# Seven products of halves for the prompt's down projection of a ConvFFN layer

## The chip, the cores and the metric

The kernel runs on one core of one Trainium2 chip. The metric is the time of one execution in device microseconds. The profile of one execution gives the span from its first to its last instruction, which is a little shorter than that time.

## The reference

The reference is one step of a hybrid attention layer, for a prompt of 1024 tokens and a sample of 32, with D_MODEL = 1024 and D_FF = 2816. All inputs and outputs are float32. What the change touches is the end of the layer, the ConvFFN with its residual:

```python
def _post_norm(x, h, gate, g, b):
    y = DEEPNORM_ALPHA * x.astype(jnp.float32) + gate.astype(jnp.float32) * h.astype(jnp.float32)
    mu = jnp.mean(y, axis=-1, keepdims=True)
    var = jnp.mean(jnp.square(y - mu), axis=-1, keepdims=True)
    return ((y - mu) * lax.rsqrt(var + LN_EPS) * g + b).astype(x.dtype)

    # in _conv_ffn
    h = jax.nn.silu(conv) * b
    return jnp.einsum('btf,fd->btd', h, w_down), a_pad[:, -(CONV_WIDTH - 1):]

    # in _layer
    f_out, conv_state = _conv_ffn(u2, conv_prev, w_up, conv_w, conv_b, w_down)
    x = _post_norm(x, f_out, g2, ln2_g, ln2_b)
```

## The kernel before

Stages follow one another: conditioning and input projection, attention, output projection with the first norm (from line 991), up projection with the convolution (from line 1071), and down projection with the second norm (from line 1115). A float32 product is made of three products of a reduced format: each operand is split into a high part (a cast on ScalarE, line 86) and a low part (a subtraction, on VectorE unless another engine is given, line 87), and `mm3` sums high x high, high x low and low x high. The profile shows these products under line 80.

The up projection writes h, transposed, into 22 tiles `hT[j]` of 128 partitions (features) and 1056 columns (1024 tokens of the prompt and 32 of the sample). Each of its 22 steps has two halves, and each half is 72 products. GpSimd (POOL) does only small copies there (lines 1087, 1088, 1093, 1094).

The down projection is `token_products("wd", ...)` (line 871). It goes through three groups of token blocks of 128, `[0, 1, 2, 8]`, `[3, 4, 5]` and `[6, 7]`, where block 8 is the sample. In each group it runs over all 22 tiles of features, and reads `w_down` anew from DRAM, 512 KB for a feature tile. `prepare` (line 880) runs two steps ahead and splits the tokens (`wdt`), the weights (`wdw`) and, in group 0, the sample (`wds`). A block of the prompt takes six products a step (two column halves of 512 by three parts), the sample four. What is left to do for a finished group (multiplying with the gate, adding the residual, statistics, scaling, storing) is handed out in pieces over the next group's steps (list `rest`). The residual, alpha x (x1 x ln1_g + ln1_b), is made in `residual` (lines 1134 to 1141): a load of x1 from the DRAM buffer `dx1`, then eight GpSimd operations of 256 columns for a block. `norm` and `scale` (lines 1146 to 1159) take VectorE, and one GpSimd power for the inverse root (`rstd`, line 978). In the last group `finish` (line 1161) shares the columns of a block among VectorE, ScalarE and GpSimd.

Each engine works through its own queue in order. A scheduler lays the order of the queues out when the program is built, from the order of the code and its own estimate of times, except in `manual_schedule` blocks, where the code's order is kept. Waits between engines are semaphores. Loads and most stores are issued by SP, in order too.

Of the kernel before, what the change touches and what calls it, by code (L numbers as in the profile page):

```python
# [51 lines left out]
def layer_kernel(ctx: ExitStack, tc: tile.TileContext, a: dict, o: list):  # L52
# [1062 lines left out]
    with pool("pf") as pf:  # L1115
# [3 lines left out]
        g2p, ag, ab, lng, lnb = [pt_(n, n, 1) for n in ("g2p", "ag", "ab", "lng", "lnb")]  # L1119
        g2s = pt_("g2s", "g2s", 1, (TS, D))  # L1120
        res = {}

        def begin2(gi, blocks):
            if gi == 0:
                for t, src in ((ag, a["ln1_g"]), (ab, a["ln1_b"]), (g2p, dgate[1][0:1]), (lng, a["ln2_g"]), (lnb, a["ln2_b"])):
                    nc.sync.dma_start(t, src.to_broadcast([P, D]))
                nc.sync.dma_start(g2s, dgate[1][1:2].to_broadcast([TS, D]))
                for t in (ag, ab):
                    nc.vector.tensor_scalar(t, t, ALPHA, None, ALU.mult)
            for b in blocks:  # L1130
                if b < NB:
                    residual(b, pt_(f"rs{b}", "rs", 3))

        def residual(b, r):
            n = rows(b)
            res[b] = r
            nc.sync.dma_start(r, dx1[b * P:b * P + n])
            for c0 in range(0, D, 256):
                c = slice(c0, c0 + 256)
                nc.gpsimd.tensor_tensor(r[:, c], r[:, c], ag[0:n, c], ALU.mult)  # L1140
                nc.gpsimd.tensor_tensor(r[:, c], r[:, c], ab[0:n, c], ALU.add)

        def evacuate2(gi, accs):
            ys, st = {}, {}

            def norm(b):
                y, n = ys[b], rows(b)
                nc.vector.tensor_tensor(y, y, res[b], ALU.add)
                st[b] = moments(y, n)

            def scale(b):
                y, n = ys[b], rows(b)
                mu, rstd = st[b]
                dst = y_p[0, b * P:(b + 1) * P] if b < NB else y_s[0]
                for h in range(2):
                    c = slice(h * 512, (h + 1) * 512)
                    nc.vector.scalar_tensor_tensor(y[:, c], y[:, c], mu, lng[0:n, c], ALU.subtract, ALU.mult)
                    nc.vector.scalar_tensor_tensor(y[:, c], y[:, c], rstd, lnb[0:n, c], ALU.mult, ALU.add)
                    nc.sync.dma_start(dst[:, c], y[:, c])

            def finish(b, acc, d):

                y = ys[b]
                st, mv = cp.tile([P, 2, 6], F32, name="st", tag="st", bufs=3), small("mv", 2, 3)
                for h in range(2):
                    c = slice(h * 512, (h + 1) * 512)
                    nc.vector.tensor_tensor(y[:, c], acc[h], g2p[:, c], ALU.mult)
                    nc.vector.tensor_tensor(y[:, c], y[:, c], res[b][:, c], ALU.add)
                    nc.vector.bn_stats(st[:, h], y[:, c])
                    yield  # L1170
                mu, rstd = spread(st, mv, P)
                nmr = small("nmr")
                nc.gpsimd.tensor_scalar(nmr, mu, rstd, -1.0, ALU.mult, ALU.mult)
                yield
                for c in (slice(0, d // 2), slice(d // 2, d)):
                    nc.vector.scalar_tensor_tensor(y[:, c], y[:, c], mu, lng[:, c], ALU.subtract, ALU.mult)
                    nc.vector.scalar_tensor_tensor(y[:, c], y[:, c], rstd, lnb[:, c], ALU.mult, ALU.add)
                    nc.sync.dma_start(y_p[0, b * P:(b + 1) * P, c], y[:, c])
                for c0 in range(d, D, 256):
                    c = slice(c0, c0 + 256)  # L1180
                    nc.scalar.activation(y[:, c], y[:, c], AF.Identity, bias=nmr, scale=rstd)
                    nc.gpsimd.tensor_tensor(y[:, c], y[:, c], lng[:, c], ALU.mult)
                    nc.gpsimd.tensor_tensor(y[:, c], y[:, c], lnb[:, c], ALU.add)
                nc.scalar.dma_start(y_p[0, b * P:(b + 1) * P, d:D], y[:, d:D])
                yield

            if gi == 2:
                steps = {}
                for b, acc in accs:
                    ys[b] = pt_(f"yo{b}", "y", 4)  # L1190
                    steps[b] = finish(b, acc, 768 if b == 7 else 256)
                with tc.manual_schedule(engines={nc.vector.engine, nc.gpsimd.engine}):
                    for b in (6, 6, 6, 7, 6, 7, 7, 7):
                        next(steps[b])
                return []
# [71 lines left out]
```

## Time and profile before

| what | us |
|---|---|
| median of 3 runs (lowest, highest) | 1599.0 (1595.2, 1604.36) |
| profiled execution, its own time | 1596.38 |
| its span, first to last instruction | 1594.1 |
| mean granted TensorE clock in it | 0.985 of full speed |
| up projection ends, down projection begins | 1297.9 |
| last product of the down projection ends | 1575.1 |

Engines are PE (TensorE), PEld (its weight loads), DVE (VectorE), ACT (ScalarE), POOL (GpSimd) and SP (which issues most transfers). Times in rows are microseconds from the start of the span, unless marked ns. A row names line, engine, operation, output <- inputs by the program's names, and shapes (partitions x columns). `x4` is a count. In square brackets stands the idle time before an instruction and what ended it. A row of windows has the stretch, its length, the busy time (and count of instructions) of PE, PEld, DVE, ACT and POOL, the granted TensorE clock, the busy share of the transfer engines and what they moved in GB/s.

### The profile page before, as it was taken

How to read it: one execution, taken by the hardware profiler on the slowest of the kernel's cores; microseconds unless marked ns; L12 is line 12 of the kernel's file. 1: busy time of each engine (PE TensorE's matmuls, PEld its weight loads, DVE VectorE, ACT ScalarE, POOL GpSimd, SP SyncE). 2: the span in 40 equal slices, each digit the busy share in tenths (PEclk: the TensorE clock that was granted, in tenths of full speed). 3: DMA queues.
4: the chain of work that ended last, by engine and by line, in shares of the span. 5: the costliest groups of instructions: out<-in, count | busy, mean ns of one | idle time of the engine just before them, and what ended most of it. 6: DMA issues, size and time to landing. Idle time of an engine off the chain costs nothing.

```text
span 1594.1 us, 22475 instructions
## 1 busy us (share of the span) xinstructions
PE 1513.3 (95%) x8657; PEld 1266.8 (79%) x8657; DVE 798.5 (50%) x1552; ACT 569.0 (36%) x1123; POOL 365.5 (23%) x496
## 2 busy tenths in 40 slices
PE   6999999988999999899899999999999999997985
PEld 4677778755646777777799999999999988876874
DVE  4522325733536899557852333233323345377495
ACT  3211211244637788545532121112111233332342
POOL 0002014744413343134300000000000005054052
PEclk9999999998999999999999999999999999999998
DMA  9523312579764433445411111111111135344362
GB/s 270 164 95 111 94 46 107 147 194 240 196 185 119 126 77 96 125 162 207 140 54 41 53 40 53 41 53 40 54 41 54 40 129 205 106 149 135 132 207 83
DMA packets 166796, 183.83 MB, mean 115 GB/s; under 512 B 7458, under 2 KB 131907, under 8 KB 166691
## 3 DMA queue, kind: packets, MB, share of 16 engines
q1 hardware_dynamic: 158642, 155.84, 32.3%
q0 software_dynamic: 7760, 26.04, 5.6%
q8 instruction: 68, 1.11, 0.3%
q10 hardware_dynamic: 288, 0.52, 0.1%
q14 instruction: 38, 0.30, 0.1%
HBM read 151.94 MB, written 22.05 MB: 109 GB/s over the span
## 4 chain that ended last, share of the span: by engine, by line
PE 80%; DVE 7%; DMA 4%; issue 2%; POOL 2%; SPq 2%; ACT 2%; POOLq 0%; DVEq 0%; ACTq 0%
PE up L80 21%; PE upc L80 10%; PE wd L80 6%; PE wo L80 4%; PE po L80 3%; PE Sf L80 2%; PE ptf L114 2%; PE Sd L80 2%; PE pod L80 1%; POOL rs L1140 1%; SPq L171 1%; PE wd2y L80 1%; PE wd2x L80 1%; DMA wrfq<-in_w_in 1%; DMA adan<-in_w_ada 1%
## 5 line engine op out<-in xcount | busy, mean ns | idle before, releaser
L1093 POOL COPY cvo<-row 128x2 f32<-128x2 f32 x22 | 20.2, 918 | 385.4 <-ACT row L1091 385.4
L86 ACT CAST wdt<-h 128x384 fp32r<-128x384 f32 (+1 forms) x66 | 31.5, 478 | 160.4 <-PE wd5y L80 70.6
L1140 POOL TENSOR_TENSOR rs<-rs,ag 128x256 f32<-128x256 f32 x32 | 40.1, 1279 | 148.3 <-DMA rs<-dx 125.5
L625 POOL TENSOR_SCALAR wf<-wf,rs 128x128 f32<-128x128 f32 (+7 forms) x64 | 47.4, 745 | 109.2 <-DVE rs L591 71.9
L87 DVE TENSOR_TENSOR wdt<-h,wdt 128x384 fp32r<-128x384 f32 (+1 forms) x66 | 36.7, 556 | 67.8 <-ACT wdt L86 67.7
L1090 ACT COPY row<-up 128x352 f32<-128x352 f32 x44 | 17.8, 458 | 135.3 <-PE up L80 135.3
L1098 ACT ACTIVATE cv<-cv 128x1058 f32<-128x1058 f32 x22 | 24.0, 1089 | 95.5 <-DVE cv L1097 95.5
L590 ACT ACTIVATE wf<-wf,lo 128x128 f32<-128x128 f32 (+7 forms) x64 | 49.5, 776 | 18.3 <-DVE lo L587 16.0
L86 ACT CAST wh<-wr 128x512 fp32r<-128x512 f32 x40 | 24.3, 621 | 85.2 <-DMA wr<-in_w_in 19.3
L590 ACT ACTIVATE wd<-wd,lo 128x128 f32<-128x128 f32 (+7 forms) x64 | 49.6, 776 | 13.9 <-DVE lo L587 11.9
L80 PE MATMUL po<-ptpf,vf 128*64 128x256 f32 (+1 forms) x320 | 53.9, 374 | 0.5 <-DVE ptpf L615 0.4
L87 DVE TENSOR_TENSOR wh<-wr,wh 128x512 fp32r<-128x512 f32 x40 | 28.6, 738 | 51.1 <-ACT wh L86 51.1
L587 DVE CUSTOM_DVE_ANT_0 wf<-Sf,nb 128x512 f32<-128x512 f32 (+3 forms) x64 | 36.9, 589 | 28.5 <-PE Sf L80 21.3
L114 PE MATMUL ptf<-cst,wf 128*128 128x128 f32 x288 | 47.8, 287 | 1.1 <-POOL wf L625 0.7
L114 PEld LDWEIGHTS ptf<-cst,wf 128*128 128x128 f32 x288 | 32.2, 144 | 18.6 <-issue 9.3
L1103 DVE TENSOR_TENSOR h<-up,cv 128x352 f32<-128x352 f32 x44 | 21.0, 520 | 45.1 <-PE up L80 44.0
L80 PEld LDWEIGHTS po<-ptpf,vf 128*64 128x64 f32 x320 | 29.0, 138 | 18.0 <-issue 6.7
L650 POOL TENSOR_SCALAR wd<-wd,rs,lam 128x128 f32<-128x128 f32 (+7 forms) x32 | 26.5, 827 | 64.4 <-DVE rs L591 63.4
L1104 DVE TENSOR_TENSOR h<-upc,cv 128x320 f32<-128x320 f32 x22 | 10.8, 492 | 57.5 <-PE upc L80 57.5
L587 DVE CUSTOM_DVE_ANT_0 wd<-Sd,zero 128x512 f32<-128x512 f32 (+3 forms) x64 | 36.6, 583 | 1.7 <-PE Sd L80 1.3
L80 PE MATMUL pod<-ptpd,vd 128*128 128x256 f32 (+1 forms) x160 | 35.2, 362 | 0.4 <-ACT sq L667 0.3
L80 PEld LDWEIGHTS pod<-ptpd,vd 128*128 128x128 f32 x160 | 29.2, 191 | 4.4 <-ACT sq L667 0.9
(2698 smaller groups left out, 5032.9 us busy)
## 6 DMA issues: line engine op xcount, KB each, us to landing
wr<-in_w_in SPq DMA_DIRECT2D x20, 512.0 KB
adam<-in_w_ada SPq DMA_DIRECT2D x32, 256.0 KB
adan<-in_w_ada SPq DMA_DIRECT2D x32, 256.0 KB
ga<-in_w_ada SPq DMA_DIRECT2D x16, 512.0 KB
out<-z POOLq DMA_DIRECT2D x12, 512.0 KB, 4.0
x<-in_x_prompt SPq DMA_DIRECT2D x8, 512.0 KB
nb<-dcump SPq DMA_DIRECT2D x8, 512.0 KB
xp<-in_x_prompt SPq DMA_DIRECT2D x8, 512.0 KB
```

The source lines that it names most:

```text
L80: nc.tensor.matmul(out, l, r, start=start, stop=stop, **k)
L86: nc.scalar.copy(hi, src)
L87: (eng or nc.vector).tensor_tensor(lo, src, f(hi), ALU.subtract)
L114: nc.tensor.transpose(out, in_, ident[:n, :n])
L587: nc.vector.tensor_tensor_reduce(w[:, c], S[:, 0:n], t, -1.0, lo, ALU.add, ALU.min, lo_)
L590: nc.scalar.activation(w[:, 0:ext], w[:, 0:ext], AF.Exp, bias=lo, scale=-1.0, accum_out=sm)
L625: nc.gpsimd.tensor_scalar(w, w, rs, 1.0, ALU.mult, ALU.mult)
L650: nc.gpsimd.tensor_scalar(e1, e1, r1, lam, ALU.mult, ALU.mult)
L1093: nc.gpsimd.tensor_copy(cvo[:, 0, :, j], row[:, T:T + 2])
L1098: nc.scalar.activation(c[:, 0:L], c[:, 0:L], AF.Silu)
L1103: nc.vector.tensor_tensor(h[:, cs], accs[g], c[:, cs], ALU.mult)
L1140: nc.gpsimd.tensor_tensor(r[:, c], r[:, c], ag[0:n, c], ALU.mult)
```

## The change

The prompt's down projection is no longer three groups of blocks over 22 feature tiles. Tokens, features and output columns are each cut in halves (512 tokens, 11 feature tiles, 512 columns), and seven products of halves (phases 0 to 6), each over 11 steps `k` and four blocks of tokens, give the four quarters of the output, with sums of halves as operands (a scheme of Winograd's kind: seven products where eight would be due). Sums of h are made on VectorE or GpSimd in six tiles `xq`, in the raw weight tiles or in place in `hT`; sums of weights are nested, each made from the one before, and kept in `hT[11 + k][:, 0:512]` (`yk`) from phase 2 on. The result's halves are collected in `y0` (tokens 0 to 511) and `y1` (512 to 1023).

The sample's 32 tokens are multiplied in phases 0, 1, 3 and 5, two products a step. After phase 4 `y0` is complete: it is gated, gets the residual (both GpSimd, 1024 columns), is normalized and stored during phase 5. After phase 5 come the parts of `y1` known by then, and the sample's end; after phase 6 `finish` for four blocks. The last three steps of phase 6 are held back and done block by block.

The residual is prepared in the up projection, in 36 steps of 256 columns by a block (one before each half from the second half on), and stored in a new DRAM buffer `dres`. The output's PSUM pool is a new one with six banks for the products and two for the sample. `token_products`, `gated` and `weights` stay for the output and up projections.

```diff
+    dres = dp.tile([TT, D], F32, name="dres")
...
+        def residuals():
+            steps = [(c0, b) for c0 in range(0, D, RW) for b in range(9)]
+            def load(i):
+                c0, b = steps[i]
+                if b == 0:
+                    gb[c0] = pe.tile([P, 2, RW], F32, name=f"gb{c0}", tag="gb", bufs=2)
+                    for x, n in enumerate(("ln1_g", "ln1_b")):
+                        nc.sync.dma_start(gb[c0][:, x], a[n][:, c0:c0 + RW].to_broadcast([P, RW]))
+                    nc.gpsimd.tensor_scalar(gb[c0], gb[c0], ALPHA, 0.0, ALU.mult, ALU.add)
+                r = pe.tile([P, RW], F32, name=f"rr{c0}{b}", tag="rr", bufs=2)[0:rows(b)]
+                nc.sync.dma_start(r, dx1[b * P:b * P + rows(b), c0:c0 + RW])
+                return r
...
+                nc.gpsimd.tensor_tensor(r, r, gb[c0][0:n, 0], ALU.mult)
+                nc.gpsimd.tensor_tensor(r, r, gb[c0][0:n, 1], ALU.add)
+                nc.gpsimd.dma_start(dres[b * P:b * P + n, c0:c0 + RW], r)
...
+    psum("psd", m=6, po=1, ms=1)
...
-        token_products("wd", w_dn, NJ, hT, begin2, evacuate2, pf, nheld=4)
...
+        LOADS = [((1, 0), None), ((1, 1), None), ((0, 1), (0, 0)), ((0, 0), None), (None, (1, 1)), ((1, 1), (0, 1)), (None, (1, 0))]
+        def load(n):
...
+            raw = (px.tile if n % 3 == 2 else pw.tile)([P, 2, 512], F32, name=f"xt{i}{k}", tag="raw", bufs=1 if n % 3 == 2 else 2)
...
+        def left(n):
...
+            if i == 0:
+                nc.vector.tensor_tensor(xq[k], hq(0, 1, k), hq(1, 1, k), ALU.add)
+                nc.gpsimd.tensor_tensor(xq[k], xq[k], hq(0, 0, k), ALU.subtract)
+        def prepare(n):
...
+            pl = px if n % 4 < 2 else pw
+            hi = pl.tile([P, 2, 512], F32R, name=f"oh{i}{k}", tag="wh", bufs=2)
+            lo = pl.tile([P, 2, 512], F32R, name=f"ol{i}{k}", tag="wl", bufs=2)
+            yk = hq(1, 0, k)
+            if i == 1:
+                nc.gpsimd.tensor_tensor(raw[:, 0], hq(1, 0, k), xq[k], ALU.subtract)
+                split(hi, lo, raw)
+            else:
+                if i == 2:
+                    nc.vector.tensor_tensor(raw[:, 0], hq(0, 1, k), hq(1, 1, k), ALU.add)
+                    nc.gpsimd.tensor_tensor(yk, raw[:, 1], x2, ALU.subtract)
+                if i in (4, 6):
+                    nc.gpsimd.tensor_tensor(yk, x2, yk, ALU.subtract)
+                if i == 5:
+                    nc.gpsimd.tensor_tensor(raw[:, 1], raw[:, 1], x2, ALU.subtract)
...
+                split(hi[:, 1], lo[:, 1], r)
+                split(hi[:, 0], lo[:, 0], l)
+                if i == 3:
+                    nc.gpsimd.tensor_tensor(l, l, hq(0, 1, k), ALU.subtract)
...
+        def gate_and_add(y, b):
+            nc.gpsimd.tensor_tensor(y, y, consts["g2p"], ALU.mult)
+            nc.gpsimd.tensor_tensor(y, y, res[b], ALU.add)
...
+        def norm(b):
+            mu, rstd = moments(y0[b], P)
+            nc.scalar.activation(y0[b], y0[b], AF.Identity, bias=nmr_of(mu, rstd), scale=rstd)
+        def scale(b):
+            y = y0[b]
+            nc.vector.tensor_tensor(y, y, consts["lng"], ALU.mult)
+            nc.vector.tensor_tensor(y, y, consts["lnb"], ALU.add)
+            nc.sync.dma_start(y_p[0, b * P:(b + 1) * P], y)
...
+        def before_last(b):
+            load_residual(4 + b)
+            gate_and_add(y1[b], 4 + b)
...
+        def finish(b, acc):
...
+            nc.vector.tensor_tensor(t, acc, consts["g2p"][:, C0], ALU.mult)
+            nc.vector.tensor_tensor(y[:, C0], y[:, C0], t, ALU.add)
+            nc.vector.bn_stats(st[:, 0], y[:, C0])
...
+            nc.scalar.activation(y[:, C1], y[:, C1], AF.Identity, bias=nmr, scale=rstd)
+            nc.gpsimd.tensor_tensor(y[:, C1], y[:, C1], consts["lng"][:, C1], ALU.mult)
+            nc.gpsimd.tensor_tensor(y[:, C1], y[:, C1], consts["lnb"][:, C1], ALU.add)
+            nc.vector.scalar_tensor_tensor(y[:, C0], y[:, C0], mu, consts["lng"][:, C0], ALU.subtract, ALU.mult)
+            nc.vector.scalar_tensor_tensor(y[:, C0], y[:, C0], rstd, consts["lnb"][:, C0], ALU.mult, ALU.add)
...
+        for i in range(NPH):
+            acc = [b1(f"wd{i}{b}", "m") for b in range(4)]
...
+            for k in range(NK):
+                n = i * NK + k
+                load(n + 3)
+                left(n)
+                prepare(n + 2)
...
+                while rest and NK * (left_ - len(rest)) < left_ * (k + 1):
+                    rest.pop(0)()
...
+                elif i in (4, 5):
+                    nc.vector.tensor_tensor(y1[b][:, C0], y1[b][:, C0], acc[b], ALU.add)
+            if i in (4, 5):
+                for b in range(4):
+                    y = (y0, y1)[i - 4]
+                    nc.vector.tensor_tensor(y[b][:, C1], y[b][:, C1], y1[b][:, C0], ALU.add)
...
+                rest += [load_consts]
+                for b in range(4):
+                    rest += [lambda b=b: gate_block(b), lambda b=b: norm(b), lambda b=b: scale(b)]
+            if i == 5:
+                rest += [lambda b=b: before_last(b) for b in range(4)] + [sample_end]
```

## Rows read from the trace of the kernel before

**Rows 1.** The page's first part: busy time, share and instructions of each engine.

```profile
PE 1513.3 (95%) x8657; PEld 1266.8 (79%) x8657; DVE 798.5 (50%) x1552; ACT 569.0 (36%) x1123; POOL 365.5 (23%) x496
```

**Rows 2.** Windows by stage: up projection, three groups of the down projection, tail.

```profile
760.00:1297.87 537.87, 533.51 (x3312) 526.97 (x3311) 202.80 (x277) 124.20 (x205) 41.48 (x104) 1.00 0.18 54
...
1297.87:1409.10 111.23, 110.12 (x486) 90.68 (x486) 53.52 (x76) 39.89 (x73) 23.89 (x24) 1.00 0.47 163
1409.10:1509.40 100.30, 91.69 (x391) 73.59 (x391) 64.96 (x84) 32.34 (x45) 36.89 (x36) 0.97 0.42 144
1509.40:1575.10 65.70, 61.25 (x265) 49.09 (x264) 58.54 (x79) 26.18 (x38) 20.83 (x20) 1.00 0.50 168
1575.10:1594.10 19.00, 2.66 (x12) 1.88 (x10) 9.21 (x16) 2.19 (x4) 8.80 (x12) 0.71 0.15 55
```

**Rows 3.** The chain in order of time, down projection: start, length, what.

```profile
1459.01 2.72 PE wd L80 x12
```

**Rows 4.** Waits in 1405:1575: who <- for whom, total, times, longest.

```profile
POOL rs L1140 <- DMA rs<-dx: 125.5, 2, 69.4
...
DVE yo L1158 <- POOL rstd L978: 11.6, 1, 11.6
...
PE wd L80 <- DVE wdw18l L87: 8.6, 1, 8.6
```

**Rows 5.** Timeline of GpSimd, undisturbed operations of 1024 and of 256 columns.

```profile
743.09 2.39 POOL L87 TENSOR_TENSOR wow17l<-wow17r,wow17h 128x1024 fp32r<-128x1024 f32 x1 [0.66 <-ACT wow17h L86]
...
1320.46 2.82 POOL L1140 TENSOR_TENSOR rs<-rs,ag 128x256 f32<-128x256 f32 x4 [22.77 <-DVE wds L87]
```

**Rows 6.** Timeline of VectorE while GpSimd is idle.

```profile
1549.09 0.42 DVE L87 TENSOR_TENSOR wdt<-h,wdt 128x256 fp32r<-128x256 f32 x1
1549.42 1.22 DVE L87 TENSOR_TENSOR wdw213l<-wdw213r,wdw213h 128x1024 fp32r<-128x1024 f32 x1
...
1569.59 0.69 DVE L1167 TENSOR_TENSOR yo<-wd6x,g2p 128x512 f32<-128x512 f32 x1 [0.83 <-PE wd6x L80]
...
1571.04 0.69 DVE L1169 BATCH_NORM_STATS2 st<-yo 128x6 f32<-128x512 f32 x1
```

**Rows 7.** Costliest groups, page: ScalarE casts of 512 columns, busy and mean ns.

```profile
L86 ACT CAST wh<-wr 128x512 fp32r<-128x512 f32 x40 | 24.3, 621 | 85.2 <-DMA wr<-in_w_in 19.3
```

**Rows 8.** Windows of three stretches in which GpSimd is busy, columns as in rows 2.

```profile
1325.60:1344.40 18.80, 18.80 (x85) 15.57 (x84) 14.01 (x14) 7.49 (x14) 18.75 (x18) 1.00 0.51 175
...
1419.90:1432.40 12.50, 12.50 (x56) 10.33 (x56) 11.15 (x20) 4.77 (x8) 12.50 (x3) 1.00 0.41 138
1442.10:1451.50 9.40, 2.48 (x11) 1.71 (x10) 8.76 (x5) 1.46 (x2) 7.56 (x12) 0.92 0.11 44
```

**Rows 9.** Groups by line in 1325.6:1344.4, VectorE and GpSimd (six splits of 1024).

```profile
L87 DVE TENSOR_TENSOR wdt<-h,wdt 128x384 fp32r<-128x384 f32 x4 | 3.1, 767 | 4.0 <-ACT wdt L86 4.0
L87 DVE TENSOR_TENSOR wds<-h,wds 128x32 fp32r<-128x32 f32 x4 | 2.9, 721 | 0.0
L87 DVE TENSOR_TENSOR wdw09l<-wdw09r,wdw09h 128x1024 fp32r<-128x1024 f32 x1 | 1.8, 1755 | 0.0
...
L1141 POOL TENSOR_TENSOR rs<-rs,ab 128x256 f32<-128x256 f32 x11 | 11.7, 1089 | 0.0
L1140 POOL TENSOR_TENSOR rs<-rs,ag 128x256 f32<-128x256 f32 x7 | 8.2, 1201 | 0.0
```

**Rows 10.** Timelines of VectorE and GpSimd, four operations stretched each.

```profile
1442.74 8.81 DVE L1158 SCALAR_TENSOR_TENSOR yo<-yo,rstd,lnb 128x512 f32<-128x512 f32 x4 [11.58 <-POOL rstd L978]
...
1418.89 13.56 POOL L1140 TENSOR_TENSOR rs<-rs,ag 128x256 f32<-128x256 f32 x4
```

**Rows 11.** Timeline of GpSimd in the tail.

```profile
1575.01 0.55 POOL L978 TENSOR_TENSOR rstd<-rstd,mhalf 128x1 f32<-128x1 f32 x1 [34.64 <-DVE rstd L977]
1575.67 0.26 POOL L1173 TENSOR_SCALAR nmr<-mv,rstd 128x1 f32<-128x1 f32 x1
...
1585.79 0.72 POOL L1183 TENSOR_TENSOR yo<-yo,lnb 128x256 f32<-128x256 f32 x1
```

More of the change, by code (lines that the diff above doesn't have):

```diff
@@ L34 @@
 BIG = 3.0e38
+RW = 256
 C_ID = 0
@@ L1074, in layer_kernel @@
         L = ROW - 2
+        def residuals():
[10 more added lines that the diff above has]
+                return r
+            gb = {}
+            nxt = load(0)
+            yield
+            for i, (c0, b) in enumerate(steps):
+                r, n = nxt, rows(b)
+                nc.gpsimd.tensor_tensor(r, r, gb[c0][0:n, 0], ALU.mult)
+                nc.gpsimd.tensor_tensor(r, r, gb[c0][0:n, 1], ALU.add)
+                nc.gpsimd.dma_start(dres[b * P:b * P + n, c0:c0 + RW], r)
+                if i + 1 < len(steps):
+                    nxt = load(i + 1)
+                yield
+        resid = residuals()
         for j in range(NJ):
@@ L1077, in layer_kernel @@
             for s in range(2):
+                if j or s:
+                    next(resid, None)
                 _, hi, lo = first_up[s] if j == 0 else up_weights(j, s)
@@ L1112, in layer_kernel @@
     up_.__exit__(None, None, None)
-    with pool("pf") as pf:
+    psum("psd", m=6, po=1, ms=1)
+    NK = NJ // 2
+    NPH = 7
+    HELD = 3
+    C0, C1 = slice(0, 512), slice(512, 1024)
+    with pool("px") as px, pool("pf") as pf:
         def pt_(name, tag, bufs, shape=(P, 1024), dt=F32):
             return pf.tile(list(shape), dt, name=name, tag=tag, bufs=bufs)
[L1119 to L1195, printed above, removed]
-            for b, acc in accs:
-                y = pt_(f"yo{b}", "y", 4)
-                ys[b] = y[0:rows(b)]
-                gated(y, b, acc, g2p if b < NB else g2s)
-                if b == 8:
-                    residual(b, g2s)
-            return [lambda b=b, g=g: g(b) for b, _ in accs for g in (norm, scale)]
-        token_products("wd", w_dn, NJ, hT, begin2, evacuate2, pf, nheld=4)
@@ new lines, in layer_kernel, with late, load_residual, load_consts @@
+        SAMPLE = {0: 0, 1: 1, 3: 0, 5: 1}
+        def late(name, shape=(P, 1024)):
+            return pt_(name, "xq", 6, shape)
+        def load_residual(b):
+            res[b] = late(f"rs{b}")
+            nc.sync.dma_start(res[b][0:rows(b)], dres[b * P:b * P + rows(b)])
+        consts = {}
+        def load_consts():
+            for n, src in (("g2p", dgate[1][0:1]), ("lng", a["ln2_g"]), ("lnb", a["ln2_b"])):
+                consts[n] = late(n)
+                nc.sync.dma_start(consts[n], src.to_broadcast([P, D]))
```

121 lines of the change are left out of this document (added).

## The prediction

> **What bounds the kernel now.** I read the page first: TensorE is busy 95% of the span [rows 1], so only less TensorE work or fewer holes in it can shorten the kernel. Then the windows by stage [rows 2]. The three groups of the down projection take 111.2, 100.3 and 65.7 us, 277.2 in all, and the tail after its last product 19.0. The chain in order of time gives the price of one product: twelve in 2.72 us, so 0.2267 us each [rows 3]. The groups hold 22 x (22 + 18 + 12) = 1144 products, 259.3 us; the other 17.9 us are holes. The waits name the largest [rows 4]: TensorE stood 8.6 us for a weight split on VectorE (wdw18l), which was queued behind a scaling that waited 11.6 us for a GpSimd result (rstd), and GpSimd was then busy with the residual (L1140). In the up projection TensorE is full (533.5 of 537.9 us) and GpSimd nearly empty (41.5) [rows 2].
>
> **TensorE's share of the change.** Seven products of 11 k steps, four blocks and three parts are 924; the sample adds 88, as before. That is 1012 products or 229.4 us, 29.9 less than now. Phases 0, 1, 3 and 5 (with the sample) have 154 products, 34.9 us each; 2, 4 and 6 have 132, 29.9 us. The loop bounds fix these counts, so that the saving itself fails is no case.
>
> **What it costs elsewhere.** Each k step splits 1024 columns (ScalarE cast, VectorE subtract) and adds a sum of 512 columns on GpSimd; phases 0 and 2 add one of 512 on VectorE. GpSimd takes 0.70 us for 256 columns and 2.39 for 1024 [rows 5], so 2.2 ns a column over a fixed 0.14, and 1.26 us for 512, a size that these rows lack. VectorE with both inputs in SBUF takes 0.42 us for 256 and 1.22 for 1024 [rows 6], 1.04 ns a column. ScalarE's two casts of 0.62 us [rows 7] lie beside a step of 2.72 us and cost nothing; if a cast comes late, the step waits those 1.24.
>
> Now the two engines together. In a stretch of 18.8 us GpSimd did 18 operations of 256 columns without a pause, and VectorE six of 1024, four of 384 and four of 32, all with two SBUF inputs [rows 8, 9]. By columns that is 4608 x 2.2 = 10.1 us and 7808 x 1.04 = 8.1 us: 18.2 of 18.8. The columns of the two did not overlap; they add. Elsewhere one engine shuts the other out: four VectorE operations of 512 columns took 8.81 us while GpSimd ran back to back, and four GpSimd operations took 13.56 us while VectorE did [rows 8, 10]. So I sum their columns as one resource, 97% filled. Operations with an input in PSUM, and the statistics, are left out of it.
>
> The Trainium skill (SBUF — State Buffer, section Who interferes with whom) states that a VectorE instruction with two SBUF inputs and a GpSimd instruction that reads SBUF exclude each other for the whole instruction. The trace agrees that they exclude each other, not that the whole duration counts: 18 x 0.70 and 6 x 1.22 alone would be 19.9 us in those 18.8. By whole durations the forecast would be 11 us longer (second rival).
>
> Phases 0 to 4: by columns, phase 0 needs 13 x 512 on GpSimd and 11 x (1536 + 32) on VectorE, 32.6 of 34.9 us; phase 2, 11 x 512 and 11 x 1536, 30.0 of 29.9. The others stay under 85%. I take 5 us of loss: 1 for the new buffers at the start (group 0 now loses 1.5 in all, 111.2 us for 484 products [rows 2]; bounds 0 and 4), 1 each in phases 0 and 2 (together 0 and 4), and 2 in all for accumulators copied out at five boundaries. There four operations of 0.69 [rows 6] meet two spare banks, six products or 1.36 us plus the 2.0 by which the first accumulator ends early; bounds 0 and 6. So phase 4 ends at 1297.9 + 164.6 + 5 = 1467.5.
>
> Phase 5: GpSimd 11 x 512 (sums) and 8 x 1024 (gate and residual of four blocks), 13,824 columns, 30.4 us; VectorE 11 x 1056 (splits), 4 x 512 (adds to y0) and 8 x 1024 (scale), 21,856 columns, 22.7 us. Together 53.1 us where TensorE has 34.9. Phase 6: GpSimd 9 x 512 and 8 x 1024, 28.2 us; VectorE 9 x 1024, 4 x 512 and 3 x 1024 for the sample's end, 14.9 us. Together 43.1 where TensorE has 29.9. The sum, 96.2, takes 99.2 at 97%, so the first accumulator of phase 6 is done at 1566.7. Here the saving goes: TensorE stands some 34 us. All of it is needed before the end, so a different order in the queues would move it, not remove it.
>
> Tail: four finishing blocks need 4 x (512 + 1024) columns on VectorE and 8 x 512 on GpSimd, 15.4 us, behind a first mult, add and statistics of 0.69 each (rows of the first and last [rows 6], the add by its columns) and a rstd and nmr of 0.55 and 0.26 [rows 11]; I take 19 us to the last GpSimd operation (bounds 16 and 24). From there to the end of the span are 7.6 us now, 1586.5 to 1594.1 [rows 2, 11]. Sum: 1566.7 + 19 + 7.6 = 1593.3, and the 2.3 us by which this execution's time stands above its span: 1596, against 1596.4 for the profiled execution, itself 2.6 under the median of 1599.0.
>
> **What moves to the up projection.** 36 steps, each with a load on SP, two GpSimd operations of 256 columns (1.4 us alone) and a store on GpSimd's queue; four times also two broadcasts on SP and one GpSimd operation. That is some 55 to 90 us of GpSimd in 538, beside 41.5 [rows 2]. SP waits for a buffer whose store began a step, 11.4 us, earlier; behind it stand the up weights, and TensorE behind those. I put 0, bounds 0 and 5. On SP in the last stage, loads of 9 x 11 x 256 KB replace 66 x 512 KB; phase 5, with two weight halves a step, constants, residuals and stores, moves some 11 MB in 54 us, 205 GB/s; the last group now has 168 at 0.50 busy [rows 2], so I expect some 0.61 and no wait. Removed from the down stage: 64 GpSimd operations of 256 columns for the residual, and with them the hole named above [rows 4].
>
> **Rivals.** *GpSimd and VectorE overlap after all, because their turns interleave*: then GpSimd's own queue bounds phases 5 and 6: 11 x 1.26 + 8 x 2.39 + 4 x 0.81 = 36.2, then 31.3. Phase 6 is done at 1535.0, and with the same tail the time is 1564. For it: statistics and PSUM operations run freely beside GpSimd. Against: [rows 8 to 10]. Chance 0.22.
> *Whole instructions exclude each other*: phases 5 and 6 are 60.8 and 49.7 us, 110.5 for 99.2; 1607. Against: [rows 8, 9]. Chance 0.07.
> *Each gate pair drains TensorE's lead* (the slower side): in phases 5 and 6 the sum of the step after next queues behind two GpSimd operations of 2.39 us, then needs 1.26, a cast of 0.62 and splits of 1.38: 8.0 us, where two steps of lead are 5.4 to 6.3. While the cast refills the pipeline both vector engines stand: about 2.5 us at each of eight pairs, 20 us, so 1616. It decides once all three loads ahead are used up when the pair begins. SP's stores of y, which wait for the scale, hold back the weight loads queued behind them in the same way. For it: the 8.6 us hole [rows 4]. Against: both engines found work all through the stretch of 18.8 us [rows 8]. Chance 0.18.
>
> **How the numbers follow.** The columns' sum has 0.53: 1596, and its own range, from the bounds of the early losses (-5, +9), of the tail (-3, +5) and a filling between 100% and 94% (-3, +3), is 1585 to 1613. About 0.5%, 8 us, is what a measurement can tell from no change, so faster is under 1591 and slower above 1607. Of the 0.53, 0.16 lies under, 0.30 within, 0.07 above. The overlap adds 0.22 to faster, the drain 0.18 to slower, whole instructions 0.03 to the same and 0.04 to slower: 0.38, 0.33, 0.29. The range for 8 in 10 takes in the overlap's 1564 and the drain's 1616: 1562 to 1616.
>
> **What would show it.** Right: phases 0 to 4 near 165 us of unbroken products; then TensorE waiting for VectorE's splits or GpSimd's sums, phase 5 over 45 us, GpSimd's 1024 columns well over 2.39 us or VectorE's 512 well over 0.69. Wrong: phases 5 and 6 near 65 us (overlap), long waits in phases 0 to 4, an up projection longer than 538 us, or SP holding loads behind a store that waits for scale.

## The result and the profile after

The change made the kernel a little slower: 1605.7 us (median of 16 runs, 1600.2 to 1613.0) beside 1594.4 us for the kernel before (16 runs), a ratio of 1.0065 [1.0046, 1.0084]. The profiled execution took 1607.87 us, its span 1606.1; before it was 1594.1.

The page's first part of the changed kernel (answers to [rows 1]):

```profile
PE 1493.1 (93%) x8525; PEld 1242.7 (77%) x8525; DVE 884.0 (55%) x1621; ACT 575.5 (36%) x1176; POOL 563.9 (35%) x635
```

TensorE lost 20.2 us of busy time, VectorE gained 85.5 and GpSimd 198.4. Where they stand is seen in the windows by stage (columns as in [rows 2]: length, then busy time of PE, PEld, DVE, ACT and POOL, granted clock, DMA share, GB/s). The first is the up projection; then come seven phases, each ended by its first accumulator being copied out, and the tail:

```profile
760.00:1298.80 538.80, 532.65 (x3296) 525.87 (x3295) 205.67 (x271) 122.48 (x201) 123.14 (x215) 0.99 0.23 69
1298.80:1341.50 42.70, 40.28 (x171) 30.93 (x169) 38.64 (x51) 15.72 (x37) 35.95 (x16) 1.00 0.32 104
1341.50:1372.50 31.00, 30.54 (x135) 25.12 (x135) 28.53 (x39) 15.02 (x30) 14.49 (x10) 1.00 0.32 107
1372.50:1412.30 39.80, 37.19 (x160) 29.39 (x158) 30.79 (x33) 18.04 (x36) 25.78 (x18) 1.00 0.55 184
1412.30:1443.70 31.40, 31.16 (x136) 25.50 (x137) 31.40 (x35) 12.13 (x26) 25.22 (x16) 1.00 0.39 133
1443.70:1471.90 28.20, 28.20 (x126) 23.35 (x125) 16.77 (x33) 14.38 (x29) 1.44 (x1) 1.00 0.38 133
1471.90:1525.80 53.90, 44.33 (x171) 33.17 (x169) 53.73 (x64) 18.31 (x35) 46.08 (x26) 0.94 0.35 123
1525.80:1570.50 44.70, 27.57 (x98) 20.80 (x99) 44.31 (x34) 10.74 (x18) 36.00 (x17) 0.81 0.25 90
1570.50:1606.10 35.60, 8.17 (x31) 4.99 (x30) 21.94 (x41) 3.15 (x4) 20.02 (x18) 0.68 0.18 66
```

Read the sixth and seventh phase (5 and 6 in the prediction, the two lines before the last): VectorE is busy 98.0 of 98.6 us, TensorE 71.9. The tail, from the reading of the last phase's first accumulator to the end, is 35.6 us; between the same two points the kernel before has 24.5 (1569.59 [rows 6] to 1594.1). The granted TensorE clock falls to 0.81 and 0.68 in the last two windows, where TensorE waits much of the time; it isn't what holds the tail up, since VectorE's readings of the four accumulators there (L1307) wait only 0.6 us for products in all. The groups of VectorE and GpSimd from 1471.9 to the end say what "busy" means there (line, operation, count, busy time, mean ns of one, idle time before):

```profile
L89 DVE TENSOR_TENSOR ol<-h,oh 128x512 fp32r<-128x512 f32 x31 | 36.2, 1201 | 0.0
L89 DVE TENSOR_TENSOR wds<-sa,wds 128x32 fp32r<-128x32 f32 x8 | 9.1, 1135 | 0.0
L1274 DVE TENSOR_TENSOR ya<-ya,lng 128x1024 f32<-128x1024 f32 x4 | 8.2, 2055 | 0.0
...
L1218 POOL TENSOR_TENSOR h<-x,h 128x512 f32<-128x512 f32 x11 | 19.8, 1824 | 1.6 <-DMA x<-in_w_down 1.6
L1258 POOL TENSOR_TENSOR yb<-yb,g2p 128x1024 f32<-128x1024 f32 x4 | 12.1, 3041 | 0.6 <-DVE yb L1380 0.6
```

A VectorE subtraction of 512 columns takes 1201 ns on average, and an add of as many takes 0.67 us in the tail below, while GpSimd is idle (L1308); one of 32 columns takes 1135 ns; GpSimd's 1024 columns take 3041 ns for 2.39 us [rows 5]. Both engines count as busy while they wait for each other (e9 below shows it). What that does to TensorE is in the waits of 1471.9 to 1570.5, the largest of PE and the largest of GpSimd on a transfer (who <- whom: total, times, longest), with the largest of SP up to 1575:

```profile
PE wd L82 <- DVE ol L89: 21.6, 9, 9.8
...
POOL yb L1259 <- DMA rs<-dres: 8.1, 1, 8.1
...
SPq L1276 <- DVE ya L1275: 30.1, 3, 14.7
```

The tail, first on VectorE and then on GpSimd (start, duration, what, idle time before):

```profile
1570.53 0.69 DVE L1307 TENSOR_TENSOR tf<-wd,g2p 128x512 f32<-128x512 f32 x1 [0.42 <-PE wd L82]
...
1571.74 0.67 DVE L1308 TENSOR_TENSOR yb<-yb,tf 128x512 f32<-128x512 f32 x1
...
1579.34 1.20 DVE L1290 TENSOR_TENSOR ys<-ys,rs 32x1024 f32<-32x1024 f32 x1
...
1582.27 0.66 DVE L1309 BATCH_NORM_STATS2 st<-yb 128x6 f32<-128x512 f32 x1
...
1594.57 1.74 DVE L1317 SCALAR_TENSOR_TENSOR yb<-yb,rstd,lnb 128x512 f32<-128x512 f32 x1 [4.34 <-POOL rstd L981]
```

```profile
1583.30 1.07 POOL L981 TENSOR_TENSOR rstd<-rstd,mhalf 32x1 f32<-32x1 f32 x1 [11.52 <-DVE rstd L980]
1584.69 1.00 POOL L981 TENSOR_TENSOR rstd<-rstd,mhalf 128x1 f32<-128x1 f32 x1 [0.33 <-DVE rstd L980]
...
1590.33 2.48 POOL L1314 TENSOR_TENSOR yb<-yb,lng 128x512 f32<-128x512 f32 x2
...
1600.34 2.48 POOL L1315 TENSOR_TENSOR yb<-yb,lnb 128x512 f32<-128x512 f32 x2
```

For 12.8 us after the first accumulator VectorE works almost alone: it does the first operations and statistics of four blocks, and the sample's end between them, while GpSimd ends its last residual and then idles 11.5 us. After that GpSimd runs 19.5 us, and VectorE's last scalings wait for it.

### The profile page after: what moved, and what is told of

Its sections match the earlier page's. It is cut to its first block, busy times and chain, and to the rows that moved or that the text cites. A ratio compares the mean times of both kernels' runs of the same rounds, so it can differ in the third digit from the quotient of the medians.

```text
span 1606.1 us, 22667 instructions
## 1 busy us (share of the span) xinstructions
PE 1493.1 (93%) x8525; PEld 1242.7 (77%) x8525; DVE 884.0 (55%) x1621; ACT 575.5 (36%) x1176; POOL 563.9 (35%) x635
## 4 chain that ended last, share of the span: by engine, by line
PE 65%; DVE 12%; DMA 10%; POOL 5%; issue 4%; SPq 2%; ACT 2%; POOLq 0%; DVEq 0%; ACTq 0%
PE up L82 15%; PE upc L82 8%; PE wd L82 7%; PE wo L82 4%; DVE ol L89 3%; PE po L82 3%; PE Sf L82 2%; DMA dres<-rr 2%; PE ptf L116 2%; DMA rr<-dx 2%; PE Sd L82 2%; DMA adan<-in_w_ada 1%; PE pod L82 1%; DMA xt<-in_w_down 1%; POOL rr L1099 1%
## 5 line engine op out<-in xcount | busy, mean ns | idle before, releaser
L82 PE MATMUL wd<-ol,oh 128*128 128x512 f32 x308 | 119.9, 403 | 17.9 <-DVE ol L89 17.9
L82 PE MATMUL wd<-oh,ol 128*128 128x512 f32 x308 | 119.5, 403 | 6.8 <-DVE ol L89 6.7
L82 PE MATMUL wd<-oh 128*128 128x512 f32 x308 | 114.0, 397 | 4.9 <-ACT oh L88 2.4
L89 DVE TENSOR_TENSOR ol<-h,oh 128x512 fp32r<-128x512 f32 x77 | 80.9, 1064 | 25.3 <-ACT oh L88 24.9
L628 POOL TENSOR_SCALAR wf<-wf,rs 128x128 f32<-128x128 f32 (+7 forms) x64 | 47.4, 745 | 109.3 <-DVE rs L594 81.7
L82 PEld LDWEIGHTS wd<-ol,oh 128*128 128x128 f32 x308 | 59.3, 193 | 33.8 <-DVE ol L89 21.6
L82 PEld LDWEIGHTS wd<-oh,ol 128*128 128x128 f32 x308 | 59.6, 194 | 22.8 <-DVE ol L89 10.8
L82 PEld LDWEIGHTS wd<-oh 128*128 128x128 f32 x308 | 59.0, 192 | 19.5 <-ACT oh L88 2.8
L88 ACT CAST oh<-h 128x512 fp32r<-128x512 f32 x77 | 46.7, 618 | 70.9 <-PE wd L82 30.6
L89 DVE TENSOR_TENSOR ol<-xt,oh 128x512 fp32r<-128x512 f32 (+1 forms) x55 | 54.8, 999 | 8.2 <-ACT oh L88 8.2
L88 ACT CAST oh<-xt 128x512 fp32r<-128x512 f32 (+1 forms) x55 | 38.8, 707 | 54.7 <-PE wd L82 31.3
L593 ACT ACTIVATE wf<-wf,lo 128x128 f32<-128x128 f32 (+7 forms) x64 | 49.5, 776 | 23.4 <-DVE lo L590 21.5
L89 DVE TENSOR_TENSOR wh<-wr,wh 128x512 fp32r<-128x512 f32 x40 | 28.6, 738 | 51.2 <-ACT wh L88 51.2
```

The source lines that it names most:

```text
L82: nc.tensor.matmul(out, l, r, start=start, stop=stop, **k)
L88: nc.scalar.copy(hi, src)
L89: (eng or nc.vector).tensor_tensor(lo, src, f(hi), ALU.subtract)
L593: nc.scalar.activation(w[:, 0:ext], w[:, 0:ext], AF.Exp, bias=lo, scale=-1.0, accum_out=sm)
L628: nc.gpsimd.tensor_scalar(w, w, rs, 1.0, ALU.mult, ALU.mult)
```

## The experiments

The changed kernel and its variants share the work ahead of the down projection, yet its first product starts anywhere from 1297.9 to 1306.6 us from one profiled execution to the next. So beside the ratio I compare the stage, from the first product to the end of the span, and its two parts, split where the first accumulator of the last phase is read (us; ratio against the kernel before, with its 95% interval; e9, e10 and e11 leave work out). A stage is that of one execution, the ratio that of several; taken from the ratios, e3 gains 7.7 us on the changed kernel where its stage gains 13.3, e9 26.6 for 31.2 and e11 2.9 for 6.4. So single stages are good to some 3 to 6 us.

| kernel | first product | to the first accumulator | from there | stage | ratio |
|---|---|---|---|---|---|
| before | 1297.7 | 271.9 | 24.5 | 296.4 | 1 |
| changed | 1299.8 | 270.7 | 35.6 | 306.3 | 1.0065 [1.0046, 1.0084] |
| e1 32 adds more | 1302.5 | 288.4 | 35.6 | 324.0 | 1.0181 [1.0140, 1.0222] |
| e2 32 statistics more | 1304.9 | 277.4 | 35.5 | 312.9 | 1.0112 [1.0080, 1.0145] |
| e3 gates on VectorE | 1299.3 | 262.7 | 30.3 | 293.0 | 1.0017 [1.0000, 1.0033] |
| e4 blocks one by one | 1300.8 | 272.5 | 36.0 | 308.5 | 1.0081 [1.0056, 1.0106] |
| e5 sample first | 1297.9 | 279.7 | 28.1 | 307.8 | 1.0086 [1.0052, 1.0121] |
| e6 stores late | 1302.0 | 270.1 | 35.6 | 305.7 | 1.0068 [1.0039, 1.0098] |
| e7 e5 and e6 | 1298.5 | 278.9 | 28.2 | 307.1 | 1.0080 [1.0050, 1.0109] |
| e9 no gates | 1305.4 | 249.2 | 25.9 | 275.1 | 0.9898 [0.9872, 0.9924] |
| e10 phase 2, one load | 1306.6 | 274.6 | 35.2 | 309.8 | 1.0088 [1.0060, 1.0115] |
| e11 no sample's end | 1304.0 | 271.4 | 28.5 | 299.9 | 1.0047 [1.0029, 1.0066] |
| e13 e5 and e4 | 1304.0 | 277.3 | 25.7 | 303.0 | 1.0063 [1.0037, 1.0088] |
| e8 residual alone | 1305.6 | 257.0 | 20.4 | 277.5 | 0.9894 [0.9858, 0.9931] |
| e12 e8, GpSimd's queue | 1298.1 | 257.0 | 23.4 | 280.3 | 0.9884 [0.9860, 0.9908] |

**Do the columns of the two engines add?** Two kernels give VectorE 32 more instructions of 512 columns, meant for the sixth phase: e1 adds with two SBUF inputs (0.67 us one, L1308 above), e2 statistics with one (0.68, L974). Their results are not used.

```diff
+ for i in range(8):                                    # behind scale(b), four times: e1 the first line, e2 the second
+     nc.vector.tensor_tensor(hq(0, 1, i), hq(0, 1, 8), hq(0, 1, 9), ALU.add)
+     nc.vector.bn_stats(hq(0, 1, i)[:, 0:6], hq(0, 1, 8 + i % 2))
```

> Changed kernel plus 32 VectorE additions of 512 columns with both inputs in SBUF, eight after each block of y0 is scaled in phase 5 (results go to a dead part of h and are not used). Times against the changed kernel, which stands 10.4 us (0.65%) above the kernel before. Theory C (in phases 5 and 6 the columns of GpSimd and of VectorE's two-SBUF-input operations add, 2.2 and 1.04 ns each): 32 x 512 x 1.04 = 17 us more, ratio to before about 1.017. Theory G (GpSimd's own queue sets the pace): 0 to 3 us more, 1.007 to 1.008. Theory V (VectorE's own busy time sets the pace, whatever it reads): 32 x 0.60 = 19 us more, 1.018.

> The same place and count, but each of the 32 extra VectorE operations is a statistics operation over 512 columns, with one SBUF input and the same 0.60 us from start to start. Theory C: these columns are not shared, 0 to 5 us more, ratio to before 1.0065 to 1.010. Theory G: 0 to 3 us. Theory V: 19 us more, 1.018, as in the run with additions.

They did not run there. Nothing that follows needs them, and the scheduler laid them far ahead of their place in the code, from the end of the third phase through the fourth (e1, then e2: duration in ns, least, median and most, then the first and last start):

```profile
L1280 DVE TENSOR_TENSOR h<-h,h x32: 673/679/1782, 1413.9 to 1464.0; 128x512 f32<-128x512 f32 x32
L1280 DVE BATCH_NORM_STATS2 h<-h x32: 669/680/696, 1414.8 to 1455.8; 128x6 f32<-128x512 f32 x32
```

So the forecasts for the sixth and seventh phase were not tested: those two take 99.9 us in e1 and 99.5 in e2, for 98.6. The pair does show something where it ran. The adds lengthened the stage by 17.7 us, 0.55 us each, the statistics by 6.6, 0.21 each, in the same place and with the same time for one. The difference is on GpSimd, whose 11 sums of the fourth phase take 2558 ns each beside the adds and 1413 beside the statistics, for 1.26 us alone (windows 1410 to 1470, e1, then e2):

```profile
L1226 POOL TENSOR_TENSOR h<-h 128x512 f32<-128x512 f32 x11 | 28.0, 2558 | 12.9 <-DVE ol L89 12.9
L1226 POOL TENSOR_TENSOR h<-h 128x512 f32<-128x512 f32 x11 | 15.5, 1413 | 11.7 <-DVE ol L89 11.7
```

VectorE is busy through the whole fourth phase in the changed kernel, e1 and e2 alike, so the 0.21 us of a statistic may be no more than its time on VectorE; that it also holds GpSimd up is not shown.

e3 moves the 16 gate and residual instructions of 1024 columns to VectorE, e9 leaves them out.

```diff
- nc.gpsimd.tensor_tensor(y, y, consts["g2p"], ALU.mult)
- nc.gpsimd.tensor_tensor(y, y, res[b], ALU.add)
+ nc.vector.tensor_tensor(...)                          # e3; e9: neither
```

> The sixteen operations of 1024 columns of gate and residual of the prompt's blocks move from GpSimd to VectorE. Theory C: 16,384 columns at 1.04 instead of 2.2 ns, 19 us less, ratio to before about 0.9945; phases 5 and 6 together near 79 us instead of 98.6. Theory G: GpSimd loses 38 of its 82 us, phases 5 and 6 fall to TensorE's 65, 30 us less, 0.988. Theory V: VectorE gains 16 x 1.14 = 18 us, 1.018.

> Left out: the gate and the residual of all eight blocks of the prompt (16 GpSimd instructions of 1024 columns; their loads stay). Theory C, the columns of GpSimd and VectorE add where both read tiles: 16 x 1024 columns at 2.2 ns, 36 us, leave the sixth and seventh phase, whose 98.6 us fall until TensorE's products (64.8 us) set them: 25 to 34 us less, ratio 0.985 to 0.991, and VectorE's splits of 512 columns take 0.7 to 0.9 us instead of 1.06. Rival V, VectorE's own list sets these phases: under 10 us less, ratio 1.000 to 1.006.

Without the gates the stage fell by 31.2 us, and the ratio of 0.9898 lies in the forecast range. But the sixth and seventh phase gave only 20.8 of it (77.8 us for 98.6, where I had forecast 25 to 34); 9.7 came from the tail. The groups show how VectorE gained (e9, 1476.8 to 1554.6, which holds both phases):

```profile
L89 DVE TENSOR_TENSOR ol<-h,oh 128x512 fp32r<-128x512 f32 x31 | 24.6, 812 | 0.0
```

The same 31 subtractions take 812 ns each for 1201: they had been waiting for the gates on another engine. With the gates on VectorE only 13.3 us of the stage came back (by the ratio 7.7), not the 19 that the columns said. The window of e3's two phases has VectorE busy 86.0 of 91.55 us, with GpSimd at 36.8. VectorE's 512 columns still take 782 ns there on average, so part of that is waiting again; what sets the pace in e3 is not shown.

```profile
1470.45:1562.00 91.55, 72.90 (x273) 52.28 (x272) 85.99 (x118) 29.00 (x53) 36.76 (x26) 0.91 0.35 118
```

**Is the order of the tail at fault?** e4 finishes the four blocks one behind the other, e5 puts the sample's end ahead of the gates of the last phase, e13 does both.

```diff
- for b in range(4):                                    # e4, e13: with its steps in this order
-     finish(b, acc[b])
+ for b in (0, 1, 0, 2, 1, 3, 2, 3):
+     next(fin[b])
- rest += [lambda b=b: before_last(b) for b in range(4)] + [sample_end]    # e5, e13
+ rest += [sample_end] + [lambda b=b: before_last(b) for b in range(4)]
```

> Only the order of VectorE's and GpSimd's queues after phase 6 is changed: the four blocks are finished one after the other (statistics and rstd of the next block, then scaling of this one), where now all statistics come before the first rstd. Theory O (the tail is long because the order makes GpSimd start when VectorE ends): the tail from the first finished accumulator to the end falls from 35.6 us to 23 to 28, ratio to before 0.999 to 1.002. Rival (the tail's columns are shared and add up whatever the order): no change, 1.0065.

> The sample's end (its multiplications, sum, statistics and scaling) is emitted ahead of the four blocks' gates of the seventh phase, instead of behind them; nothing else differs. Theory T, the sample's end sits in VectorE's queue between the first accumulator and the four blocks' ends and makes the tail of 32.3 us (forecast 19): the tail falls to 21 to 25 us and the ratio to 0.999 to 1.002. Rival B, the tail is long because VectorE and GpSimd hand each block's end to each other: the tail stays at 29 to 33 us, ratio 1.005 to 1.007. Rival L, the sample's loads stand behind the stores of the first four blocks in SP's queue, so VectorE now waits for them in the middle of the phase: the tail is short but the first accumulator comes 5 to 15 us later, ratio 1.006 to 1.010.

> The sample's end ahead of the gates of the seventh phase, and the four blocks finished one behind the other (each block's GpSimd work beside the next block's VectorE work). Theory O, the order is what makes the tail long, and the two changes of it that gave nothing alone stood in each other's way: the stage from the first product to the end falls from 306.3 to 292 to 299 us, ratio 0.997 to 1.002. Theory W, what VectorE and GpSimd have to do in the last two phases and the tail is done one after the other in any order: the stage stays at 304 to 310 us, ratio 1.004 to 1.010, with a shorter tail and a later first accumulator.

Not by much. e4 left the tail at 36.0; in it VectorE did the sample's end after the first block, and waited 3.2 us for the sample's sum on TensorE. e5 cut the tail by 7.5 us, and the first accumulator came 9.0 us later, with VectorE busy 106.0 of the last 107.5 us ahead of it. e13 cut it by 9.9 and paid 6.6: its stage of 303.0 lies 3.3 under the changed kernel's, between the bounds that I had set for order and for amount, and its ratio of 1.0063 is that of the changed kernel. So order is worth at most some 3 us. In e13 the two engines do work side by side on different blocks, and each block still takes 4.6 us, of which their columns make 3.9. GpSimd in the tail of e13, two blocks' first instruction:

```profile
1591.75 0.98 POOL L981 TENSOR_TENSOR rstd<-rstd,mhalf 128x1 f32<-128x1 f32 x1
...
1596.33 0.99 POOL L981 TENSOR_TENSOR rstd<-rstd,mhalf 128x1 f32<-128x1 f32 x1
```

e11 leaves out the sample's gate, residual, statistics and scaling.

```diff
- nc.vector.tensor_tensor(y[0:TS, c], ps[0:TS], gs[:, c], ALU.mult)
+ nc.scalar.copy(y[0:TS, c], ps[0:TS])
- ...                                                   # residual, moments and scaling
```

> Left out: the sample's gate, residual, statistics and scaling (7.2 us of VectorE and one GpSimd instruction; the sum over TensorE, the loads and the store stay). Theory W, work on VectorE and GpSimd adds up to the end, whatever its order: the tail of 32.3 us falls to 23 to 26 us and the kernel by 6 to 9, ratio 1.001 to 1.003. Rival O, the tail is GpSimd's own chain of four blocks behind the last statistics, and the sample's end lies beside TensorE's last products: under 3 us, ratio 1.0045 to 1.0075.

The part behind the first accumulator fell by 7.1 us (GpSimd's last instruction ends 25.2 us after the first accumulator, for 32.3), the stage by 6.4. By the ratio it is about 3 us, with intervals that meet, and 1.0047 lies at the edge of the rival's range, not in that of theory W. So the run speaks for the amount of work in its profile, and leaves it open in its time.

**Do SP's stores cost anything?** In the changed kernel a store of y0 that waits for its scaling holds a residual load, and GpSimd idles 8.1 us (above). e6 is meant to issue those four stores last; e7 adds the sample's end first.

```diff
- nc.sync.dma_start(y_p[0, b * P:(b + 1) * P], y)
+ stores.append(lambda: nc.sync.dma_start(y_p[0, b * P:(b + 1) * P], y))   # run behind sample_end
```

> The stores of the first four blocks are issued by SP behind the last residual loads instead of ahead of them. Theory S, a store that waits for its block's scaling holds the residual loads behind it (28.89 us in the chain of waits, and 8.07 us in which GpSimd waits for a residual): the seventh phase gets 5 to 8 us shorter and so does the kernel, ratio 1.0015 to 1.0035. Rival C, VectorE's and GpSimd's columns set the phase whenever the loads land: within 2 us of the changed kernel, ratio 1.005 to 1.0075.

> Both together: the sample's end first, the stores of the first four blocks last. If both theories hold, the tail falls by 8 to 11 us and the seventh phase by 5 to 8 us: ratio 0.994 to 0.999. If only the order of the sample counts: 0.999 to 1.002. If neither: 1.005 to 1.0075.

Their stages are 305.7 us for 306.3 and 307.1 for e5's 307.8, but theory S was not tested. In e6 the scheduler left the stores where they were: SP waits for the last three and issues the residual load behind them, and GpSimd idles 7.9 us for it as before.

```profile
1538.82 27.23 SPq L1276 DMA_DIRECT2D out<-ya  x3
1566.10 0.43 SPq L1248 DMA_DIRECT2D rs<-dres  x1
```

In e7 two of the stores still stand ahead of the last three residual loads, as in e5. What the held load costs stays open. The 8.1 us are not all lost: while GpSimd idles, VectorE's subtractions run at 0.6 us each (six in 3.69 us from 1564.02), for 2.8 us beside the gates.

**Why does the third phase lose 10 us?** e10 leaves out one of the two loads of each step there.

```diff
- if LOADS[i][1]:
+ if LOADS[i][1] and i != 2:
- nc.gpsimd.tensor_tensor(yk, raw[:, 1], x2, ALU.subtract)
+ nc.gpsimd.tensor_tensor(yk, raw[:, 1], hq(0, 0, k), ALU.subtract)
```

> Left out: one of the two weight loads of each step in the third phase (a half of h stands in for it, so that the sum has the same columns). Theory L, GpSimd's sums wait there for loads whose buffers come free late, 19.3 us in 7 waits: the third phase falls from 39.8 to 31 to 34 us, and the kernel by 6 to 9, ratio 1.001 to 1.003. Rival C, columns fill that phase (30.0 of 29.9 us): it stays over 37.5 us, ratio 1.005 to 1.0075.

The phase stayed, 40.4 us. Its window and a piece of GpSimd's timeline:

```profile
1379.10:1419.50 40.40, 36.97 (x151) 28.83 (x150) 40.18 (x35) 17.28 (x34) 31.52 (x20) 0.96 0.48 148
```

```profile
1384.02 1.74 POOL L1218 TENSOR_TENSOR h<-x,h 128x512 f32<-128x512 f32 x1
1385.73 1.74 POOL L1216 TENSOR_TENSOR h<-xt,h 128x512 f32<-128x512 f32 x1
...
```

L1218 is the sum of the fifth phase: in the instruction streams its sums run two phases early, in turn with the third phase's own. In e10 the phase so holds 20 GpSimd and 32 VectorE instructions of 512 columns, 22.5 + 17.0 = 39.5 us by columns, and VectorE is busy 40.18 of its 40.40 us. In the changed kernel they are 18 and 31, 36.8 of 39.8 us, where I had counted 11 and 33; GpSimd waits there for loads (11.0 us), and the fifth phase has one GpSimd instruction left. Without one load more sums ran ahead and filled the phase, so the columns set its length in e10. In the changed kernel they leave 3.0 us for the loads and all else.

**What is each half of the change worth?** e8 is the kernel before with the residual prepared in the up projection, and no nested products; e12 the same with that preparation's loads on GpSimd's queue. The products without the moved residual weren't tried.

```diff
+ resid = residuals()                                   # e8: in the up projection, as in the change
- nc.sync.dma_start(r, dx1[b * P:b * P + n])
- ...                                                   # 4 x (multiply by ag, add ab) on GpSimd
+ nc.sync.dma_start(r, dres[b * P:b * P + n])
- nc.sync.dma_start(r, dx1[b * P:b * P + rows(b), c0:c0 + RW])
+ nc.gpsimd.dma_start(r, dx1[b * P:b * P + rows(b), c0:c0 + RW])          # e12; the broadcasts too
```

> The kernel before, with only the second part of the change: the residual is multiplied and shifted by GpSimd in the up projection and kept in memory, and the down projection loads it. Theory C, the engines' columns add wherever both read tiles, so the down projection is relieved of 64 GpSimd instructions: TensorE's holes there (17.9 us) shrink, 3 to 12 us less, ratio 0.9925 to 0.998. Rival N, TensorE bounds that projection and the holes are not GpSimd's: ratio 0.9985 to 1.001. Rival U, the added GpSimd work delays VectorE in the up projection and nothing comes back: 1.001 to 1.005.

> The kernel before with the moved residual alone, its loads issued on GpSimd's queue instead of SP's. Theory H, on SP they stand behind stores that have to end first (115.5 us of waits) and hold the up weights: some 4 us of TensorE's holes between 760 and 1000 us go, ratio 0.985 to 0.989 where it was 0.9894. Rival G, GpSimd pays for issuing them and nothing changes: 0.989 to 0.992.

The residual alone takes 14.9 us off the part up to the first accumulator, in e8 and e12 alike, more than my range; of the rest of the stage, 4.1 and 1.1 us less in two kernels with the same code there, little is certain. The kernel is 1.1% faster than before. The seven products then put 26 to 29 us on (277.5 or 280.3 to 306.3; by the ratios 27 and 29), about half of it up to the first accumulator and half behind. A window of e12 that holds its second group and the start of its third shows the holes gone:

```profile
1406.50:1509.00 102.50, 102.50 (x448) 82.99 (x447) 71.39 (x98) 34.38 (x48) 9.92 (x4) 1.00 0.50 161
```

TensorE is busy all of it (second group before: 91.69 of 100.30), with GpSimd at 9.92 us for 36.89. Between 900 and 1000 us TensorE is busy 97.42 us in e8 and 100.00 in e12, so the loads on SP did hold the up weights; e8 and e12 can't be told apart by their ratios. e12 has the best ratio of the study, and both it and e8 beat both kernels.

## Why the prediction was wrong

I forecast 1596 us, no change; it is slower by 0.65%, just past the 0.5% bound and inside the range. **The step that failed is the tail**: "I take 19 us to the last GpSimd operation (bounds 16 and 24)" measured 32.3, from 1570.5 to 1602.8. The other terms, in their order:

- First product: forecast 1297.9, found 1299.8. "I put 0, bounds 0 and 5" for the up projection holds (window 538.8 us for 537.9, GpSimd at 123.1 in it, for 41.5 plus the 55 to 90 forecast).
- Phases 0 to 4: forecast 169.6, found 172.1. The sum was near, its parts were not: phase 2 took 39.8 us and phase 4 28.2, because sums ran ahead (e10).
- Phases 5 and 6: forecast 99.2 us at 97%, found 98.6. That it met so well is in part luck: the sample's end had moved into the tail and two sums ahead of the phases, so the columns that ran in the 98.6 us are 90.6, not 96.2, and fill 92% of them, less than the 94% that I had as a bound. GpSimd's and VectorE's columns do add. One stretch of the changed kernel shows it again: from 1540.14 to 1561.20 GpSimd did seven instructions of 1024 columns and VectorE two of 1024 and six of 512. By columns that is 15.8 + 5.3 = 21.1 us, and the stretch has 21.06. By their durations alone it would be 7 x 2.39 + 2 x 1.22 + 6 x 0.67 = 23.2, or 22.6 with VectorE's 0.60 and 1.14 from start to start.
- Tail: 13.3 us too long. From the last GpSimd operation to the end: 3.3 us for 7.6; this part is 3.1 in e8 and 6.0 in e12, with one code, so its size is no term to count on. All together 12.8 us of span (1606.1 for 1593.3).

```profile
1540.65 3.39 DVE L1274 TENSOR_TENSOR ya<-ya,lng 128x1024 f32<-128x1024 f32 x1
1543.97 3.42 DVE L1380 TENSOR_TENSOR yb<-yb 128x512 f32<-128x512 f32 x2
1547.32 3.35 DVE L1275 TENSOR_TENSOR ya<-ya,lnb 128x1024 f32<-128x1024 f32 x1
1550.60 12.36 DVE L89 TENSOR_TENSOR ol<-h,oh 128x512 fp32r<-128x512 f32 x6
```

```profile
1540.14 6.10 POOL L1258 TENSOR_TENSOR yb<-yb,g2p 128x1024 f32<-128x1024 f32 x2
1546.87 6.00 POOL L1258 TENSOR_TENSOR yb<-yb,g2p 128x1024 f32<-128x1024 f32 x2 [0.63 <-DVE yb L1380]
1552.83 8.37 POOL L1259 TENSOR_TENSOR yb<-yb,rs 128x1024 f32<-128x1024 f32 x3
```

These are the two timelines of that stretch, VectorE's (of the six L89 three lie in it whole and the fourth but for its last 0.6 us; as much of an L1380 begun earlier lies at its start) and GpSimd's.

What the tail term left out: I counted the columns of four blocks, 15.4 us, one block's first operations, 2.1, and one rstd and nmr, 0.8 [rows 11]. In the trace VectorE first does those operations of all four blocks and the sample's end, 12.8 us where I had 2.1 (the sample's end I had put into phase 6, at 3.2; without it the part to the last GpSimd instruction is 7.1 us shorter, e11). Then GpSimd's nine rstd and nmr of one column take 9.1 us where I had 0.8, and eight instructions of 512 columns 10.1; alone the nine would take 3.8. Against that, VectorE's part of my 15.4, 6.4 us, was done before those instructions or beside them.

Phases 5, 6 and tail together, from 1471.9 to 1602.8, took 130.9 us, and my two terms made 118.2. The columns of the two engines that ran in that time are 109.3 us, as forecast (96.2 + 15.4 = 111.6, less the 2.2 of the two sums). So the mis-sized term is all that lies beside the columns: 21.6 us, where I had allowed 6.6. It holds what I had put at almost nothing with "Operations with an input in PSUM, and the statistics, are left out of it", and the one-column instructions; how the 15 us divide among them and waits is not settled. The runs leave little to order (e13: 3.3 us of the stage, nothing of the ratio).

The rival *whole instructions exclude each other* gave 1607, near the result, but for another reason: it had 110.5 us for phases 5 and 6, which took 98.6, and the stretch above holds 22.6 to 23.2 us of whole instructions in 21.06. The Trainium skill (SBUF — State Buffer, SBUF: two separate sides) states that a VectorE instruction with two SBUF inputs and a GpSimd instruction that reads SBUF exclude each other for the whole instruction; this stretch agrees that they exclude each other, not that the whole durations add. The overlap, which had 67.5 us for phases 5 and 6, falls with their 98.6, and with e9, where VectorE's subtractions speed up once the gates are gone. The drain by gate pairs had VectorE and GpSimd stand some 20 us in these phases; TensorE does wait 21.6 us for L89, but VectorE is busy 98.0 of the 98.6 us, and the columns alone fill 90.6 of them, which leaves no room for 20 us of standing. That a store held on SP costs time is not refuted: it delays a residual by 8.1 us, and no run took it away.

The signs that I named for being right came: phase 5 at 53.9 us, GpSimd's 1024 columns at 3041 ns, VectorE's 512 at 1201. So did signs for being wrong: phase 2 was 10 us longer than its products, with waits for loads and sums; SP held a load behind stores that wait for the scaling; and the up projection, at 538.8 us, stood just above 538.

A second thing that my total hid: I netted the products' saving against the holes of the kernel before, and named only one hole for the residual. e8 and e12 show that the move of the residual is worth 14.9 us up to the first accumulator, so most of the 17.9 us of holes were the residual's. On a kernel without those holes the products cost 26 to 29 us. Only with the gates left out altogether, which e8 still does, is their stage (275.1 us, e9) as short as e8's (277.5).

## What to carry to other kernels

When a change trades TensorE's work for vector work, sum VectorE's and GpSimd's columns of everything up to the end as one resource, the last blocks included, and give statistics, PSUM operations and one-column instructions a term of their own: here they and the waits were 21.6 us of 130.9. An order of the tail changed little of that. Price the two halves of a change apart: here one half won 1.1%, and the other lost more than that. A busy share of 98% on an engine may be waiting: compare the mean of one instruction with its time beside an idle neighbour. And look in the trace where an added instruction or a moved transfer has landed before reading its time: the scheduler ran e1's and e2's two phases early and left e6's stores where they were.
